# A right factor's cast and its difference given separate places in the order of work

## The chip, the cores and the metric

The kernel runs on one core of a Trainium2 chip. The metric is the time of one execution in device microseconds (us). One execution was also taken with the hardware profiler; its rows are in microseconds from the start of its span. PE is TensorE (matmuls), PEld its weight loads, DVE is VectorE, ACT is ScalarE, POOL is GpSimd and SP is SyncE.

## The reference, cut to what matters

A decoder layer in float32, on x of 1 x 512 x 2048: four token mixers with gates and an output projection, then an MLP of width 8192. The change lies in the MLP.

```python
def mlp(h, g, w_up, w_down):            # condensed; h: 512 x 2048
    y = rms_norm(h, g)
    u = jnp.square(jax.nn.relu(y @ w_up))   # 2048 -> 8192
    return h + u @ w_down                   # 8192 -> 2048
```

## The kernel before, in words

**Products.** Each float32 matmul is done as three products of rounded parts: of every operand there is a high part (a cast to the matmul's format) and a low part (the operand less its high part). `mm3` issues high by high, low by high and high by low (line 173, 128x128 weights by 128x256).

**Pairs.** The large multiplications use seven products of half size in place of eight (Winograd's form of Strassen's method). A *pair* makes one 256-row block of the result's channels from eight *keys* (pieces of the contraction), in seven products, in the order 1, 6, 7, 4, 5, 2, 3; a product is 8 keys x 3 = 24 matmuls. Four banks of PSUM, a to d, take the products: 1 in a, 6 in b, 7 in c, 4 in b again, 5 in d, then 2 on top of a, and 3 on top of d. VectorE adds each bank into the results when it is done (`add`, line 933: `ud<-pdb,y` reads product 6 out of bank b, `ud<-pdc` product 7, then into `y`), and ScalarE copies bank a (line 951). Product 4 can't start in b before `ud<-pdb,y` has been done.

**Left factors** are the weights: DMAs issued by SyncE bring quarters (`wq`), VectorE forms the method's sums (`z`, line 671), ScalarE casts them (`uh`, line 713) and VectorE makes the low part (`ul`, line 719). Each has three buffers.

**Right factors** are the activations, one of 7 x 256 columns for each key. `hi` is a cast on ScalarE (`sh`, line 886), `lo` a difference on VectorE (`sl`, line 890); `parts_of` returns the two steps. In up, the factors of keys 0 to 7 are made once, and hold for all 32 pairs. Up's results go through `hidden` (scale and ReLU on VectorE, square on ScalarE, four sums `token_sums` on VectorE at lines 858 to 861) and are written to memory as `zd` by GpSimd's DMA queue, as down's right factors. Down's pair n uses keys n to n + 7, so each pair needs one new right factor; it is fetched back (`std<-zd`, from GpSimd's queue) and made one pair ahead of its use, into one of nine slots. The next fetch is issued right behind the difference.

**Duos.** The first and the last two pairs of up and the first two of down go in two halves of the contraction (`run_duo`), so that keys 0 to 3 (of both pairs) come before keys 4 to 7. There, products share groups and left factors are 128x512.

**The order.** The order in which instructions are written is the order in which each engine runs them. `step` runs one product, and ahead of it what the planner gives: the cast of the left factor two products on, then all tasks from the list `later` that are due and marked `must`, then the difference of that left factor; then the product's matmuls; the reading of its bank is put in the list `pending` and comes at the next step. `wait_for(fn, n, after, must)` puts a task in `later`, due `after` microseconds on the planner's own clock, which goes by the matmuls planned. If a product needs a right factor that isn't made, `flush` takes the tasks in the order of their times until it is. The fetch of a later key's factor into slot 8 and the pair results share room in memory with the duos' results: slot 8's low part lies where the second pair's result `y1` was, which a GpSimd DMA adds to `x1d` (line 1325).

```python
    def in_parts(key, src, after=0.0, must=False, then=None):
        first, second = parts_of(key, src)
        ...
        wait_for(first, 0, after, must)
        wait_for(last, 7 * H, after, must)
    ...
    def place_down(J, after, following):
        in_parts(("d", J), staged[J], after, True, lambda: fetch_down(following))
    ...
            renew((n + 8,), (1.4,), (n + 9,))
```

Of the kernel before, what the change touches and what calls it, by code (L numbers as in the profile page):

```python
# [98 lines left out]
def body(nc, tc, ctx, dram):  # L99
# [25 lines left out]
    def t512(tag, name, dt=F32, rows=P):  # L125
        return stage[tag].tile([rows, S], dt, name=name, tag=tag, bufs=BUFS[tag])

    def bank(name, tag="mm"):
        return psum.tile([P, 512], F32, name=name, tag=tag, bufs=4)
# [109 lines left out]
    def pc(name, i=0, rows=P):  # L239
        c = _COLS[name][0] + i  # L240
        return par[:rows, c : c + 1]
# [369 lines left out]
    H = 256  # L611
# [139 lines left out]
    def spend(n):  # L751
        busy[0] += (0.06 + n / 960) / 1.09
# [19 lines left out]
    def wait_for(fn, n=0, after=0.0, must=False):  # L772

        later.append((clock[0] + after, n, fn, era[0], must))
# [23 lines left out]
    def result(name, where, tag, cols):  # L798

        for t in list(later):  # L800
            if t[3] < era[0]:
                pop(t)
        era[0] += 1
        return wide(name, where, tag, 2, cols)
# [49 lines left out]
    def token_sums(t):  # L854


        b11, b12, b21, b22, t2, t3, t4 = (t[:, q * H : (q + 1) * H] for q in range(7))
        V.tensor_tensor(out=t3, in0=b22, in1=b12, op=ALU.subtract)
        V.tensor_tensor(out=b12, in0=b12, in1=b11, op=ALU.subtract)
        V.tensor_tensor(out=t2, in0=b22, in1=b12, op=ALU.subtract)  # L860
        V.tensor_tensor(out=t4, in0=b21, in1=t2, op=ALU.subtract)
# [14 lines left out]
    def parts_of(key, src):  # L876


        def first():
            slot = slot_of(key)  # L880
            hi, lo = (
                spools[slot][1].tile([P, 7 * H], F32R, name=f"s{q}{key[0]}{key[1]}", tag=f"s{q}{slot}", bufs=1)
                for q in "hl"
            )
            place[key] = (hi, lo)
            A.copy(hi, src)  # L886

        def second():
            hi, lo = place[key]
            V.tensor_tensor(out=lo, in0=src, in1=f(hi), op=ALU.subtract)  # L890
            right[key] = (hi, lo)

        return first, second

    def in_parts(key, src, after=0.0, must=False, then=None):
        first, second = parts_of(key, src)

        def last():
            second()
            if then:  # L900
                then()

        wait_for(first, 0, after, must)
        wait_for(last, 7 * H, after, must)

    def fetch(key, where):

        t = wide(f"st{key[0]}{key[1]}", *where)
        G.dma_start(t, zd[key[0]][key[1] % UP])
        return t  # L910

    def wide(name, where, tag, bufs, cols=7 * H):
        return where[1].tile([P, cols], F32, name=name, tag=tag, bufs=bufs)

    def half_wide(name, where):
        return wide(name, where, "u", 1, S)
# [11 lines left out]
    def blocks(out, u):  # L928
        return [out[:, q * H : (q + 1) * H] for q in range(4)] + [u[:, :H], u[:, H:]]
# [69 lines left out]
    for k in range(4):  # L999
# [51 lines left out]
        for j in range(8):  # L1051
            for e, ps in rows(f"branch{k}", 0, j, yk, f"pb{k}"):
                n = 2 * j + e
# [56 lines left out]
    def gate_tiles(n):  # L1110
        j, k = GATES[n]
        return result(f"g{k}_{j}", gpool, "r", 1024), half_wide(f"u{k}_{j}", gpool)

    for n, phase in enumerate(gate_pairs):
        g, u = gate_tiles(n)
# [44 lines left out]
    for e in range(2):  # L1160
        hi, lo = (t512("q", f"mg{q}{7 + 8 * e}", F32R) for q in "hl")
        src = merged[0][:, e * S : (e + 1) * S]
# [9 lines left out]
    factors = {}  # L1172

    def add_in(out, a, b):
        V.tensor_tensor(out=out, in0=a, in1=b, op=ALU.add)

    def residual(n, ps):

        j, e = n % 8, n // 8
        r = t512("r", f"x1_{n}")  # L1180
        G.dma_start(r, dram["xT"][n])

        def first():
            spend(S)
            add_in(r, ps, r)
            G.dma_start(x1d[j][:, e * S : (e + 1) * S], r)
            wait_for(scaled, S, 0, n == 15)
            wait_for(square)

        def square():  # L1190
            sq = acc if n == 0 else t512("g", f"sq{n}")
            A.activation(sq, r, AF.Square)
            if n:
                wait_for(lambda: add_in(acc, acc, sq), S)

        def scaled():
            if e == 0:
                factors[j] = wide(f"x2_{j}", *((st1, "st1", 1) if j % 2 else (opool, "o", 1)))
            o = factors[j]
            V.scalar_tensor_tensor(  # L1200
                out=o[:, e * S : (e + 1) * S], in0=r, scalar=pc("g_mlp", n), in1=p, op0=ALU.mult, op1=ALU.mult,
            )
            if e:
                wait_for(sums, 4 * 300, 0, j == 7)

        def sums():
            token_sums(factors[j])
            if j < 4:
                in_parts(("u", j), factors[j])
            elif j < 6:  # L1210
                G.dma_start(zd["u"][j], factors[j])
            elif j == 7:
                in_parts(("u", 6), factors[6], 0, True)
                in_parts(("u", 7), factors[7], 5, True)

        return [first]

# [18 lines left out]
    last = {n: bank(f"pw{n}") for n in (7, 15)}  # L1236
# [28 lines left out]
    def up_tiles(n):  # L1265
        return result(f"h{n}", upool[0], "o", 7 * H), half_wide(f"uu{n}", upool[0])

    def hidden(n, o):
        up_scale = scale[1]
        if n == 0:  # L1270
            finish(scale[0])
            V.tensor_tensor(out=up_scale, in0=up_scale, in1=n2[1], op=ALU.mult)

        def scaled(e):
            r = o[:, e * S : (e + 1) * S]
            V.scalar_tensor_tensor(out=r, in0=r, scalar=0.0, in1=up_scale, op0=ALU.max, op1=ALU.mult)

        def sums():
            token_sums(o)
            G.dma_start(zd["d"][n], o)  # L1280

        for e in range(2):
            wait_for(lambda e=e: scaled(e), S)
        wait_for(lambda: A.activation(o[:, R], o[:, R], AF.Square))
        wait_for(sums, 4 * 300)
# [8 lines left out]
    staged = {}  # L1294

    def fetch_down(J):
        if J < UP + 7:
            staged[J] = fetch(("d", J), (upool[0], "s", 1) if J % 2 and J < 10 else ST1)

    def place_down(J, after, following):  # L1300
        in_parts(("d", J), staged[J], after, True, lambda: fetch_down(following))

    def renew(keys, times, following):
        for J, t, m in zip(keys, times, following):
            wait_for(lambda J=J, m=m: place_down(J, 0, m), 0, t, True)

    for n, phase in enumerate(up_pairs, 2):
        o, u = up_tiles(n)
# [2 lines left out]
            fetch_down(1)  # L1311
        run_pair(phase, o, u)
        hidden(n, o)
    TIMES = (0, 2.5, 11, 15)
    run_duo(
        up_last, [lambda n=n: up_tiles(n) for n in (UP - 2, UP - 1)],
        lambda: renew((0, 1, 2, 3), TIMES, (2, 3, 4, 5)),
        [lambda o, n=n: hidden(n, o) for n in (UP - 2, UP - 1)],
# [4 lines left out]
    def put(n, r):  # L1323
        q = n % 8
        G.dma_start(x1d[q], r, accum_op=ALU.add)
        if n >= UP - 8:
            for e in range(2):
                nc.sync.dma_start(dram["out"][q + 8 * e], x1d[q][:, e * S : (e + 1) * S])

    renew((4, 5, 6, 7), TIMES, (6, 7, 8, 9))  # L1330
    run_duo(
# [9 lines left out]
    for n, phase in enumerate(down_pairs, 2):  # L1341
        r, u = result(f"y{n}", dpool, "r", 1024), half_wide(f"ud{n}", dpool)
        if n + 1 < UP:
            renew((n + 8,), (1.4,), (n + 9,))
            run_pair(phase, r, u)
            pending.append(lambda n=n, r=r: put(n, r))
            continue
        x1 = wide("x1r", *ST1)[:, R]
        G.dma_start(x1, x1d[n % 8])
        x11, x12, x21, x22, _, _ = blocks(x1, u)  # L1350
        c11, c12, c21, c22, u2, u3 = blocks(r, u)

        def out(e, sl):
            nc.sync.dma_start(dram["out"][n % 8 + 8 * e][:, sl], r[:, e * S : (e + 1) * S][:, sl])

        run_pair(phase, r, u, {
            7: lambda: add_in(u2, u2, x12),
            4: lambda: add_in(c21, c21, x21),
            5: lambda: (add_in(c22, c22, x22), out(1, slice(0, S))),
            2: lambda: (add_in(c11, c11, x11), out(0, slice(0, H))),  # L1360
            3: lambda: out(0, slice(H, S)),
        })
# [77 lines left out]
```

## Time and profile before

| | |
|---|---|
| median of 3 runs | 2805.49 us (2804.15 to 2807.04) |
| the profiled execution's own time | 2807.36 us |
| its span, first to last instruction | 2805.6 us |
| mean granted TensorE clock | 0.993 |
| PE, PEld busy | 2722.6 us (97%), 2547.5 us (91%) |
| DVE, ACT, POOL busy | 2162.5 us (77%), 1229.7 us (44%), 180.4 us (6%) |

A busy share is an average over stages. In a row of the timeline stand the start, the duration, the engine, the line, the operation, what it writes and reads without buffer numbers, its shape, and in square brackets how long the engine had been idle and what ended that. The MLP's up begins at about 1452 us, down at about 2090, and down's steady pairs run from about 2206 to the end.

### The profile page before, as it was taken

The page shows a single profiled execution, that of the slowest core. Times are in us where ns is not written, and L with a number is a line of the kernel's source. Part 1 is how long each engine was busy: PE and PEld are TensorE (multiplying, and loading weights), DVE is VectorE, ACT ScalarE, POOL GpSimd, SP SyncE. Part 2 cuts the span into 40 slices and gives each one's busy share as a digit, 9 for nine tenths or more (in the row PEclk, how much of TensorE's full clock was granted, in tenths as well). Part 3 has the DMA queues.
Part 4 walks back from the last instruction along what each step waited for, and adds up shares of the span by engine and source line. Part 5 has one row for each costly group of instructions (what it writes and reads, how often), then busy time and mean ns, then how long its engine had stood idle before and what let it go on. Part 6 is the DMA issues. An engine that isn't in the chain of part 4 may idle for free. (4 is left out here: it accounts for less than half of the span.)

```text
span 2805.6 us, 48202 instructions
## 1 busy us (share of the span) xinstructions
PE 2722.6 (97%) x19904; PEld 2547.5 (91%) x19904; DVE 2162.5 (77%) x2664; ACT 1229.7 (44%) x1520; POOL 180.4 (6%) x298
## 2 busy tenths in 40 slices
PE   8999999999999999999999999999997999999999
PEld 7787777789999999998879999999997899999999
DVE  6875655577888888886559898888888787787786
ACT  5443334554444444443234444444444444444443
POOL 3000000000000000012100000000000000000000
PEclk9999999999999999999999999999998999999999
DMA  5232223564444444456444444444445555655564
GB/s 177 93 98 79 88 67 116 195 221 146 156 143 156 145 151 136 144 174 224 157 137 171 146 158 158 153 159 146 164 159 180 159 178 162 174 174 164 172 206 136
DMA packets 143901, 429.49 MB, mean 153 GB/s; under 512 B 16696, under 2 KB 30904, under 8 KB 143680
## 3 DMA queue, kind: packets, MB, share of 16 engines
q1 hardware_dynamic: 101536, 279.19, 29.5%
q0 software_dynamic: 32496, 129.65, 16.0%
q10 hardware_dynamic: 9648, 17.57, 1.7%
q8 instruction: 156, 2.56, 0.4%
q14 instruction: 65, 0.53, 0.1%
HBM read 350.04 MB, written 79.97 MB: 153 GB/s over the span
## 5 line engine op out<-in xcount | busy, mean ns | idle before, releaser
L713 ACT CAST uhd<-wqd 128x1024 fp32r<-128x1024 f32 (+3 forms) x136 | 135.4, 998 | 220.0 <-PE pdd L173 76.0
L713 ACT CAST uhg<-wqg 128x1024 fp32r<-128x1024 f32 (+1 forms) x136 | 135.6, 1000 | 185.3 <-PE pgd L173 96.4
L713 ACT CAST uhu<-wqu 128x1024 fp32r<-128x1024 f32 (+1 forms) x144 | 136.2, 952 | 163.5 <-PE pud L173 86.7
L151 DVE TENSOR_TENSOR wl<-wr,wh 128x1024 fp32r<-128x1024 f32 (+2 forms) x100 | 121.6, 1219 | 90.3 <-ACT wh L150 86.4
L719 DVE TENSOR_TENSOR ulg<-wqg,uhg 128x1024 fp32r<-128x1024 f32 (+1 forms) x136 | 157.1, 1158 | 33.4 <-ACT uhg L713 33.4
L713 ACT CAST uhd<-zd 128x1024 fp32r<-128x1024 f32 (+3 forms) x102 | 102.0, 1000 | 159.0 <-PE pdb L173 95.5
L150 ACT CAST wh<-wr 128x1024 fp32r<-128x1024 f32 (+2 forms) x100 | 101.1, 1014 | 160.3 <-PE pb L173 34.1
L719 DVE TENSOR_TENSOR uld<-wqd,uhd 128x1024 fp32r<-128x1024 f32 (+3 forms) x136 | 157.1, 1158 | 17.8 <-ACT uhd L713 17.8
L713 ACT CAST uhg<-zg 128x1024 fp32r<-128x1024 f32 (+1 forms) x102 | 102.0, 1000 | 150.0 <-DVE ulg L719 103.3
L173 PE MATMUL pdb<-shd,uhd 128*128 128x256 f32 x480 | 137.8, 287 | 30.0 <-DVE ud L933 30.0
L890 DVE TENSOR_TENSOR sld<-std,shd 128x1792 fp32r<-128x1792 f32 x39 | 78.9, 2025 | 111.9 <-ACT shd L886 105.8
L719 DVE TENSOR_TENSOR ulu<-wqu,uhu 128x1024 fp32r<-128x1024 f32 (+1 forms) x144 | 157.8, 1101 | 9.1 <-ACT uhu L713 9.0
L713 ACT CAST uhu<-zu 128x1024 fp32r<-128x1024 f32 (+1 forms) x108 | 103.1, 955 | 128.7 <-DVE ulu L719 69.0
L173 PE MATMUL pdb<-shd,uld 128*128 128x256 f32 x480 | 135.7, 283 | 0.0
L173 PE MATMUL pdb<-sld,uhd 128*128 128x256 f32 x480 | 135.6, 282 | 0.0
L173 PE MATMUL pda<-shd,uld 128*128 128x256 f32 x480 | 134.7, 281 | 0.8 <-DVE uld L719 0.8
L173 PE MATMUL pdd<-shd,uhd 128*128 128x256 f32 x480 | 134.6, 280 | 0.0
L173 PE MATMUL pdd<-shd,uld 128*128 128x256 f32 x480 | 134.5, 280 | 0.0
L173 PE MATMUL pda<-sld,uhd 128*128 128x256 f32 x480 | 134.5, 280 | 0.0
L173 PE MATMUL pda<-shd,uhd 128*128 128x256 f32 x480 | 134.5, 280 | 0.0
L173 PE MATMUL pdd<-sld,uhd 128*128 128x256 f32 x480 | 134.5, 280 | 0.0
L173 PE MATMUL pgb<-shg,ulg 128*128 128x256 f32 x480 | 134.2, 280 | 0.0
(1462 smaller groups left out, 10522.8 us busy)
## 6 DMA issues: line engine op xcount, KB each, us to landing
wqg<-in_w SPq DMA_DIRECT2D x120, 512.0 KB, 3.5
wqu<-in_w SPq DMA_DIRECT2D x112, 512.0 KB, 3.5
wr<-in_w SPq DMA_DIRECT2D x84, 512.0 KB, 3.5
std<-zd POOLq DMA_DIRECT2D x39, 896.0 KB, 4.8
zd<-h POOLq DMA_DIRECT2D x32, 896.0 KB, 4.8
bk<-b ACTq DMA_DIRECT2D x64, 256.0 KB, 2.8
b<-bk POOLq DMA_DIRECT2D x32, 512.0 KB, 4.6
wo<-in_w SPq DMA_DIRECT2D x32, 512.0 KB, 3.5
```

Of the source, the lines that this page charges most:

```text
L150: A.copy(hi, raw)
L151: V.tensor_tensor(out=lo, in0=raw, in1=f(hi), op=ALU.subtract)
L173: T.matmul(out, w, x, start=start, stop=stop, skip_group_check=more)
L713: A.copy(self.hi[:, sl], self.phase.source(i))
L719: V.tensor_tensor(out=lo, in0=self.phase.source(i), in1=f(hi), op=ALU.subtract)
L890: V.tensor_tensor(out=lo, in0=src, in1=f(hi), op=ALU.subtract)
```

## The change

`in_parts` gets an argument `apart`: the difference is due so much later than the cast. For down's right factors and up's last two it is 1, so that the difference comes one step after the cast. Up's keys 6 and 7 are made 2 us later (2 and 7 in place of 0 and 5), and the sums ahead of them as well. In down's first duo the last of four factors is due at 13 in place of 15. In pair 2 the new factor (key 10) is due at 9 in place of 1.4.

```diff
-    def in_parts(key, src, after=0.0, must=False, then=None):
+    def in_parts(key, src, after=0.0, must=False, then=None, apart=0.0):
...
         wait_for(first, 0, after, must)
-        wait_for(last, 7 * H, after, must)
+        wait_for(last, 7 * H, after + apart, must)
...
             if e:
-                wait_for(sums, 4 * 300, 0, j == 7)
+                wait_for(sums, 4 * 300, 2 if j == 7 else 0, j == 7)
...
             elif j == 7:
-                in_parts(("u", 6), factors[6], 0, True)
-                in_parts(("u", 7), factors[7], 5, True)
+                in_parts(("u", 6), factors[6], 2, True, None, 1)
+                in_parts(("u", 7), factors[7], 7, True, None, 1)
...
-        in_parts(("d", J), staged[J], after, True, lambda: fetch_down(following))
+        in_parts(("d", J), staged[J], after, True, lambda: fetch_down(following), 1)
...
-    TIMES = (0, 2.5, 11, 15)
+    TIMES = (0, 2.5, 11, 13)
...
         if n + 1 < UP:
-            renew((n + 8,), (1.4,), (n + 9,))
+            renew((n + 8,), (9 if n == 2 else 1.4,), (n + 9,))
```

No engine gets more or fewer instructions. Three places show what moves; a name's last number is a running one, and the one before it (if there are two) the key or the product.

VectorE in a steady pair (14) of down, before. `uld14_7`, `uld14_4` and `uld14_5` are the low parts of the left factors of products 7, 4 and 5; `sld22` is the right factor's difference:

```order
L719 TENSOR_TENSOR uld14_7_24941<-wqd14_0_1_24837,uhd14_7_24940 128x1024
L890 TENSOR_TENSOR sld22_24975<-std22_24744,shd22_24974 128x1792
L719 TENSOR_TENSOR uld14_4_24971<-wqd14_0_2_24840,uhd14_4_24970 128x1024
L933 TENSOR_TENSOR ud14_24935<-pdb_24937,y14_24934 128x256
L719 TENSOR_TENSOR uld14_5_25006<-zd14_1_24843,uhd14_5_25005 128x1024
L933 TENSOR_TENSOR ud14_24935<-pdc_24938,ud14_24935 128x256
```

VectorE in the same pair after the change:

```order
L719 TENSOR_TENSOR uld14_7_24941<-wqd14_0_1_24837,uhd14_7_24940 128x1024
L719 TENSOR_TENSOR uld14_4_24971<-wqd14_0_2_24840,uhd14_4_24970 128x1024
L933 TENSOR_TENSOR ud14_24935<-pdb_24937,y14_24934 128x256
L890 TENSOR_TENSOR sld22_24975<-std22_24773,shd22_24974 128x1792
L719 TENSOR_TENSOR uld14_5_25003<-zd14_1_24843,uhd14_5_25002 128x1024
L933 TENSOR_TENSOR ud14_24935<-pdc_24938,ud14_24935 128x256
```

The difference stands behind the low part for product 4 and the reading of bank b, and still ahead of the low part for product 5; the cast on ScalarE stays where it was.

VectorE in pair 2, the first whole pair of down, before:

```order
L719 TENSOR_TENSOR uld2_7_22139<-wqd2_0_1_22052,uhd2_7_22138 128x1024
L890 TENSOR_TENSOR sld10_22171<-std10_21859,shd10_22170 128x1792
L719 TENSOR_TENSOR uld2_4_22167<-wqd2_0_2_22055,uhd2_4_22166 128x1024
L933 TENSOR_TENSOR ud2_22133<-pdb_22135,y2_22132 128x256
L719 TENSOR_TENSOR uld2_5_22202<-zd2_1_22058,uhd2_5_22201 128x1024
```

VectorE there after the change:

```order
L719 TENSOR_TENSOR uld2_7_22139<-wqd2_0_1_22052,uhd2_7_22138 128x1024
L719 TENSOR_TENSOR uld2_4_22167<-wqd2_0_2_22055,uhd2_4_22166 128x1024
L933 TENSOR_TENSOR ud2_22133<-pdb_22135,y2_22132 128x256
L719 TENSOR_TENSOR uld2_5_22196<-zd2_1_22058,uhd2_5_22195 128x1024
L933 TENSOR_TENSOR ud2_22133<-pdc_22136,ud2_22133 128x256
L671 TENSOR_TENSOR zd2_2_22084<-wqd2_0_3_22226,zd2_2_22084 128x1024
L719 TENSOR_TENSOR uld2_2_22225<-wqd2_0_3_22226,uhd2_2_22224 128x1024
L933 TENSOR_TENSOR y2_22132<-pdb_22135,ud2_22133 128x256
L671 TENSOR_TENSOR zd3_1_22270<-wqd3_0_1_22264,wqd3_0_2_22267 128x1024
L719 TENSOR_TENSOR uld2_3_22258<-zd2_2_22084,uhd2_3_22257 128x1024
L933 TENSOR_TENSOR y2_22132<-pdd_22137,ud2_22133 128x256
L890 TENSOR_TENSOR sld10_22262<-std10_21908,shd10_22261 128x1792
```

Key 10's difference goes from the place behind product 7's low part to behind the reading of bank d after product 5; its cast moves on ScalarE in the same way, and GpSimd's fetch for key 11 follows it.

VectorE ahead of the second half of down's first duo, which begins with key 4 and takes key 7 for the first time, before. `h30` and `h31` are up's last two results, `sld7` is key 7's difference:

```order
L861 TENSOR_TENSOR h30_21287<-h30_21287 128x256
L890 TENSOR_TENSOR sld7_21818<-std7_21617,shd7_21817 128x1792
L671 TENSOR_TENSOR zd0_1_21737<-wqd0_0_2_21734,zd0_1_21737 128x512
L719 TENSOR_TENSOR uld0_5_21814<-zd0_1_21737,uhd0_5_21813 128x512
L719 TENSOR_TENSOR uld0_5_21814<-wqd0_0_2_21734,uhd0_5_21813 128x512
L933 TENSOR_TENSOR ud0_21812<-pd6_21566,y0_21811 128x256
```

VectorE there after the change:

```order
L861 TENSOR_TENSOR h30_21287<-h30_21287 128x256
L671 TENSOR_TENSOR zd0_1_21737<-wqd0_0_2_21734,zd0_1_21737 128x512
L719 TENSOR_TENSOR uld0_5_21817<-zd0_1_21737,uhd0_5_21816 128x512
L719 TENSOR_TENSOR uld0_5_21817<-wqd0_0_2_21734,uhd0_5_21816 128x512
L1276 SCALAR_TENSOR_TENSOR h31_21425<-h31_21425,ups_14263 128x512 x2
L858 TENSOR_TENSOR h31_21425<-h31_21425 128x256
L859 TENSOR_TENSOR h31_21425<-h31_21425 128x256
L860 TENSOR_TENSOR h31_21425<-h31_21425 128x256
L861 TENSOR_TENSOR h31_21425<-h31_21425 128x256
L890 TENSOR_TENSOR sld7_21795<-std7_21655,shd7_21794 128x1792
L933 TENSOR_TENSOR ud0_21815<-pd6_21566,y0_21814 128x256
```

The difference of key 7 goes behind a sum and two low parts of the left factors and behind h31's scaling and sums, and h31's work comes ahead of where it was.

## The prediction

> **What bounds the kernel now.** I read the page first, then TensorE's waits, then windows by stage, and last the rows of one pair on each engine. From the page:
>
> ```profile
> span 2805.6 us, 48202 instructions
> ...
> PE 2722.6 (97%) x19904; PEld 2547.5 (91%) x19904; DVE 2162.5 (77%) x2664; ACT 1229.7 (44%) x1520; POOL 180.4 (6%) x298
> ```
>
> TensorE is busy for 97% of the span, so no reordering can win more than the 83.0 us (2805.6 − 2722.6) in which it idles, and what it runs at half clock behind idle stretches. Its waits (line waited for, total us, times, longest):
>
> ```profile
> PE pdb L173 <- DVE ud L933: 30.0, 29, 5.2
> PE pu L173 <- DVE ulu L719: 12.4, 7, 3.8
> ```
>
> The largest is VectorE's reading of bank b in down's pairs, 29 times. Up's and down's steady stretches as windows (start:end, length, then busy us of PE, weight loads, VectorE, ScalarE, GpSimd, granted clock, DMA share, GB/s):
>
> ```profile
> 1530.00:2060.00 530.00, 529.78 (x4520) 529.58 (x4519) 469.93 (x597) 237.91 (x273) 14.88 (x28) 1.00 0.47 158
> 2206.00:2785.00 579.00, 555.07 (x4655) 550.34 (x4655) 454.27 (x473) 257.54 (x275) 38.89 (x55) 1.00 0.59 174
> ```
>
> In up VectorE is busy for 89% and TensorE never waits; in down VectorE has less to do (78%), and TensorE idles for 23.9 us. So the lack is one of order. One steady pair (14) on the four engines (start, us, operation, idle before):
>
> ```profile
> 2429.38 0.28 PE L173 MATMUL pdb<-shd,uhd 128*128 128x256 f32 x1
> 2432.22 0.28 PE L173 MATMUL pdc<-shd,uhd 128*128 128x256 f32 x1
> 2436.09 0.36 PE L173 MATMUL pdb<-shd,uhd 128*128 128x256 f32 x1 [0.87 <-DVE ud L933]
> ...
> 2429.51 1.05 ACT L713 CAST uhd<-wqd 128x1024 fp32r<-128x1024 f32 x1 [1.78 <-PE pda L173]
> ...
> 2430.72 1.69 ACT L886 CAST shd<-std 128x1792 fp32r<-128x1792 f32 x1
> ...
> 2427.76 1.23 DVE L719 TENSOR_TENSOR uld<-wqd,uhd 128x1024 fp32r<-128x1024 f32 x1 [0.58 <-ACT uhd L713]
> 2432.44 2.02 DVE L890 TENSOR_TENSOR sld<-std,shd 128x1792 fp32r<-128x1792 f32 x1 [3.46 <-ACT shd L886]
> 2434.39 1.22 DVE L719 TENSOR_TENSOR uld<-wqd,uhd 128x1024 fp32r<-128x1024 f32 x1
> 2435.52 0.42 DVE L933 TENSOR_TENSOR ud<-pdb,y 128x256 f32<-128x256 f32 x1
> 2435.85 1.22 DVE L719 TENSOR_TENSOR uld<-zd,uhd 128x1024 fp32r<-128x1024 f32 x1
> ```
>
> TensorE runs product 6 into bank b from 2429.38, product 7 into c from 2432.22, and wants b again for product 4 at 2435.05 (2432.22 plus 2.83, below). Bank b is full at about 2432.2, but VectorE reads it (ud<-pdb) only at 2435.52: it waited 3.46 us for the cast of the right factor, then made that factor's difference (2.02) and uld4 (1.22). ScalarE does the cast (shd) last of its work there, so VectorE idles in front of an operation that nobody needs before the next pair.
>
> **The change, part by part.**
>
> *Down's steady pairs, 3 to 30.* The stalls in question, first and last of 28, and the last pair, which makes no right factor (chain of waits):
>
> ```profile
> 2205.80 0.36 PE L173 MATMUL pdb<-shd,uhd 128*128 128x256 f32 x1 [0.88 <-DVE ud L933]
> 2770.87 0.36 PE L173 MATMUL pdb<-shd,uhd 128*128 128x256 f32 x1 [0.88 <-DVE ud L933]
> ...
> 2785.30 2.83 PE pdb L173 x24
> ...
> 2799.47 2.84 PE pdd L173 x24
> ```
>
> A pair now takes (2770.87 − 2205.80)/27 = 20.93 us. Without a stall it takes seven products of (2799.47 − 2785.30)/5 = 2.834, so 19.84: 1.09 less (0.88 of idle, the rest in the slower products behind it). Afterwards uld4 and ud<-pdb stand ahead of the difference. I replay it: uld7 runs from 2427.76 as now; uld4 follows its cast, done at 2430.56, and ends by about 2431.8; ud<-pdb goes at about 2432.4, when bank b is full; the difference at 2432.75, as shd ends at 2432.41; uld5 behind it is done by 2435.9. Product 4 starts at 2435.05 unhindered; product 5, which needs uld5, at 2437.9 and would need the low part some 0.2 us on: 2.2 us to spare. That is what is late next, and it isn't late. The moved step also issues the next fetch of std on GpSimd's queue; it comes 0.3 us later in its pair, at about 2435.1, some 15 us before the next cast wants it (2430.72 + 19.84). Ends: nothing gained (the wait moves to uld5), and, with up's 530.00/4520 = 0.1173 us a matmul, 168 of them in 19.70, 1.23 a pair. I take the last pair's, which runs the same instructions: 28 × 1.09 = 30.5 us (0 to 34.4).
>
> *Pair 2, the first whole pair of down.* Here the wait is longer, since slot 8's low part lies on a buffer that the adding DMA of the previous result still reads (rows of VectorE and PE, the window behind the wait, and the fetch of a factor with its count, size and median us to landing):
>
> ```profile
> 2178.69 2.03 DVE L890 TENSOR_TENSOR sld<-std,shd 128x1792 fp32r<-128x1792 f32 x1 [6.06 <-DMA x1d<-y]
> 2182.33 0.55 PE L173 MATMUL pdb<-shd,uhd 128*128 128x256 f32 x1 [5.19 <-DVE ud L933]
> 2187.59 0.41 PE L173 MATMUL pdd<-shd,uhd 128*128 128x256 f32 x1
> 2182.30:2188.00 5.70, 5.67 (x26) 5.70 (x27) 3.79 (x5) 0.34 (x1) 0.00 (x0) 0.50 0.86 297
> ...
> std<-zd POOLq DMA_DIRECT2D x39, 896.0 KB, 4.8
> ```
>
> The stall costs 5.19, and product 4 behind it takes 5.26 (2187.59 − 2182.33) in place of 2.83, at a granted clock of 0.50: 5.19 + 2.43 = 7.6 us. Product 1 of this pair began at 2168.7 (2182.33 − 5.19 − 3 × 2.83), so that DMA was done 10.0 into it. With 9 in place of 1.4 the difference of key 10 goes behind product 5, from 14.6 to 16.6 (5 × 2.83, a reading of 0.42, 2.02), when the DMA is long done. The next key's fetch then goes out at 17.0 and lands at 21.8; its cast wants it at 24.0 (19.84 + 4.2, as in pair 14), so 2 us are to spare. Ends: 0 and 8.2; I take 7.6. The Trainium skill, "TensorE: Matmul & The Clock Gate", section "What's actually happening", holds that an idle window of about 3.4 us halves the clock until a window has been busy. By that rule the loss behind the stall is half a window, 1.7 us, so the term would be 6.9 and the sum 0.7 smaller; the trace agrees on the 0.50 but shows 2.43, and the row decides.
>
> *Down's first duo, and up's last (2058 to 2171).* Waits on TensorE, and what held them (a window first):
>
> ```profile
> 2126.00:2136.00 10.00, 3.21 (x18) 2.42 (x16) 8.84 (x12) 5.00 (x7) 1.06 (x2) 0.70 0.51 183
> ...
> 2133.83 0.58 PE L173 MATMUL pd<-shd,uhd 128*128 128x256 f32 x1 [2.69 <-ACT shd L886]
> 2135.89 0.58 PE L173 MATMUL pd<-sld,uhd 128*128 128x256 f32 x1 [1.48 <-DVE sld L890]
> 2152.73 0.38 PE L173 MATMUL pd<-shd,uhd 128*128 128x256 f32 x1 [1.11 <-ACT uhd L713]
> 2157.11 0.58 PE L173 MATMUL pd<-shd,uld 128*128 128x256 f32 x1 [3.88 <-DVE uld L719]
> ...
> 2130.11 1.06 ACT L1284 ACTIVATE h<-h 128x1024 f32<-128x1024 f32 x1
> ...
> 2133.81 2.03 DVE L890 TENSOR_TENSOR sld<-std,shd 128x1792 fp32r<-128x1792 f32 x1 [0.73 <-ACT shd L886]
> 2154.30 2.03 DVE L890 TENSOR_TENSOR sld<-std,shd 128x1792 fp32r<-128x1792 f32 x1
> 2158.49 0.37 ACT L979 COPY y<-pd 128x256 f32<-128x256 f32 x1 [3.60 <-DMA zd<-h]
> ```
>
> Three things happen. Key 7's difference (2133.81) is needed by the second half's first product. It falls behind two uld, h31's two scalings, ScalarE's square of h31 (as the 1.06 of h30) and four sums; since all of it is needed at once, 13 in place of 15 doesn't help. These operations run some 2.4 us earlier than now, and by my count of their durations the difference ends at about 2137.4 in place of 2135.84, 1.5 later. Key 9's difference (2154.30) no longer stands ahead of uld1_7, so 3.88 and 1.11 fall away; and h31's factor is written earlier, so the copy no longer waits 3.60. The 2.4 is what the same shift wins in the duo parts ahead. In all I get +5.1 for the start of pair 2; what then limits is the weights' DMA into pair 2. Ends: −4, if key 7's lateness costs a stretch at half clock as in pair 2 and the later gains are swallowed; +14, if all these waits go.
>
> *Up's first duo.*
>
> ```profile
> 1457.06 0.38 PE L173 MATMUL pu<-shu,ulu 128*128 128x256 f32 x1 [1.24 <-DVE ulu L719]
> 1464.03 0.39 PE L173 MATMUL pu<-shu,ulu 128*128 128x256 f32 x1 [3.76 <-DVE ulu L719]
> 1468.18 2.02 DVE L890 TENSOR_TENSOR slu<-x,shu 128x1792 fp32r<-128x1792 f32 x1 [1.67 <-ACT shu L886]
> 1471.47 0.38 PE L173 MATMUL pu<-shu,ulu 128*128 128x256 f32 x1 [1.40 <-DVE ulu L719]
> ```
>
> Here slu6 and slu7 go 2 us later, behind the left factors that TensorE waits for. The three waits are 6.4 us; the same differences must be made before the second half, so half comes back: +3.0, between −1 and +6.9.
>
> Sum: 30.5 + 7.6 + 5.1 + 3.0 = 46.2 us. The profiled execution took 2807.36 us, 1.8 over its span; that gives 2761.2. It stands 1.87 above the median of the runs, 2805.49, so on their scale 2759.
>
> **The rivals.**
>
> *Key 7 goes worse than I count* (chance 0.15). Its difference now waits for h31's square and sums; TensorE idles up to 10 us there, and runs the next products at 0.50. The first duo's term is then −4: gain 37, 2768. For it: 5.19 of idle in pair 2 cost 2.43 behind it. Against: that stretch idles now too: 3.21 us busy in 10, clock 0.70.
>
> *The wait moves to uld5* (0.10). If the difference starts later than I replay, by more than 2.2 us, product 5 waits for uld5. At half of the old price a pair keeps 0.5: 14 us less gain, 2773. For it: VectorE has no pause from 2432.44 on, so each delay reaches uld5. Against: the 2.2 us, more than the difference itself takes.
>
> *All of it goes* (0.08): products at up's 0.1173 a matmul and the duos at their upper ends: 34.4 + 8.2 + 8 + 5 = 56, 2750. For it: up's pairs run so with VectorE busier. Against: the last pair, with no difference in it, ran at 2.834.
>
> *Slower: the right factor's fetch comes late* (0.03). In each pair ScalarE's cast of std stands ahead of the cast of uhd5; if std hasn't landed, ScalarE and then TensorE stand.
>
> ```profile
> DVE sld L890 <- ACT shd L886: 105.8, 35, 3.5
> ```
>
> Against it: the fetch lands 4.8 us after its issue, and 35 of VectorE's waits in front of the difference end on the cast. The cast would have to come 2.5 us later for a stall, and 4.2 (2.5, the 1.09 saved, and 16/28 for the other terms) for the kernel to be slower than before: std landing about 20 us after its issue (2435.1 to 2454.8). It is issued on GpSimd while VectorE works without a gap; the Trainium skill, "SBUF — State Buffer", section "SBUF: two separate sides", has VectorE and GpSimd share one port pair as an exclusive lock, which could hold up such an issue, and no run here shows it doing so.
>
> *No change* (0.02): the order shows the differences behind ud<-pdb; only a wait not in the trace could undo that.
>
> **How the numbers follow.** The forecast has 0.62: 2759, by itself 2752 to 2765 (the ends of the two duos). The range for 8 in 10 reaches on one side to the rival "all of it", 2749, and on the other past key 7's and half into uld5's, 2773. Faster by over 0.2% (5.6 us, about what a measurement of this kernel can tell) holds all cases but the last two: 0.95; same 0.02, slower 0.03.
>
> **What would show it.** Right: TensorE's wait on ud at L933 falls from 29 times 30.0 us to under 3; VectorE's idle time in front of sld falls from 105.8; a steady pair takes 19.8 to 19.9. Pair 2 shows no granted clock of 0.50. Key 7's sld ends later against the start of its half, and the wait for it grows. Wrong: waits on uld at L719 in every pair (then the second rival), or on uhd at L713 behind a late std.

## The result, and the profile after

The changed kernel takes 2759.56 us (median of 4 runs, 2758.59 to 2761.39), the kernel before 2804.82 (4 runs, 2804.07 to 2807.04): a ratio of 0.9834, 95% interval 0.9821 to 0.9847, 45.3 us less. The forecast was 2759. From the page of the profile after:

```profile
span 2756.7 us, 48177 instructions
...
PE 2709.0 (98%) x19904; PEld 2540.5 (92%) x19904; DVE 2163.2 (78%) x2664; ACT 1229.9 (45%) x1520; POOL 180.8 (7%) x298
```

The counts of instructions are the same on every engine and the busy times nearly so; the span is 48.9 us shorter. TensorE's longest waits after the change, then two of VectorE's (waited for, total us, times, longest):

```profile
PE pd L173 <- DVE sld L890: 11.1, 2, 10.3
PE pu L173 <- DVE ulu L719: 9.9, 5, 4.0
...
PE pd L173 <- DVE uld L719: 2.3, 4, 1.0
...
DVE ud L933 <- ACT shd L886: 18.4, 28, 0.7
...
DVE sld L890 <- ACT shd L886: 0.7, 1, 0.7
```

The line that headed the list before, bank b's reading with 30.0 us in 29 waits, is gone, and VectorE's idle time in front of the difference has fallen from 105.8 us to 0.7. New at the top is one wait of 10.3 us on `sld`: key 7's. The steady stretch as a window, and a steady pair on PE, ScalarE and VectorE:

```profile
2180.00:2733.00 553.00, 552.83 (x4690) 552.63 (x4689) 457.48 (x474) 261.11 (x279) 39.52 (x56) 1.00 0.63 185
...
2404.89 0.29 PE L173 MATMUL pdb<-shd,uhd 128*128 128x256 f32 x1
...
2400.56 1.70 ACT L886 CAST shd<-std 128x1792 fp32r<-128x1792 f32 x1
...
2400.42 1.23 DVE L719 TENSOR_TENSOR uld<-wqd,uhd 128x1024 fp32r<-128x1024 f32 x1 [1.60 <-ACT uhd L713]
2402.31 0.42 DVE L933 TENSOR_TENSOR ud<-pdb,y 128x256 f32<-128x256 f32 x1 [0.66 <-ACT shd L886]
2402.77 2.02 DVE L890 TENSOR_TENSOR sld<-std,shd 128x1792 fp32r<-128x1792 f32 x1
2404.71 1.22 DVE L719 TENSOR_TENSOR uld<-zd,uhd 128x1024 fp32r<-128x1024 f32 x1
```

TensorE now idles for 0.2 us in 553. VectorE reads bank b at 2402.31, and product 4 starts in it at 2404.89, with no idle time in its row. (The "0.66 <-ACT shd" before `ud<-pdb` is time in which VectorE waits for bank b to fill; the row names what ended about then.) The difference goes next, without a wait, and the low part for product 5 ends at 2405.93 (2404.71 plus 1.22), 2.0 us ahead of the matmul that takes it first, at 2407.95.

Where the 48.9 us are, by the starts of the first matmul into each stage's banks in the two traces:

| stage | before | after | gained | forecast |
|---|---|---|---|---|
| ahead of up | 1452.60 | 1451.16 | 1.4 | 0 |
| up's first duo | 50.08 | 47.42 | 2.7 | 3.0 |
| up's pairs | 555.61 | 555.48 | 0.1 | 0 |
| up's last and down's first duo | 109.14 | 103.58 | 5.6 | 5.1 |
| pair 2 | 28.82 | 20.85 | 8.0 | 7.6 |
| pairs 3 to 30 | 586.04 | 554.96 | 31.1 | 30.5 |
| pair 31 and after | 23.3 | 23.3 | 0 | 0 |

The profile of before was at the long end of its runs and that of after at the short end, so the two traces differ by some 3.5 us more than the medians do. The 1.4 us ahead of up are not the change's: in the twelve profiles of this document, whose code there is the same, up starts between 1450.3 and 1453.1 us. Down's first matmul is at 2104.86 us in the trace of before and at 2100.88 in that of after.

### The profile page after: what moved, and what is told of

It is laid out like the page before. It is cut to its first block, busy times and chain, and to the rows that moved or that the text cites. A ratio compares the mean times of both kernels' runs of the same rounds, so it can differ in the third digit from the quotient of the medians.

```text
span 2756.7 us, 48177 instructions
## 1 busy us (share of the span) xinstructions
PE 2709.0 (98%) x19904; PEld 2540.5 (92%) x19904; DVE 2163.2 (78%) x2664; ACT 1229.9 (45%) x1520; POOL 180.8 (7%) x298
## 5 line engine op out<-in xcount | busy, mean ns | idle before, releaser
L713 ACT CAST uhg<-wqg 128x1024 fp32r<-128x1024 f32 (+1 forms) x136 | 135.6, 999 | 185.3 <-PE pgd L173 96.4
L173 PE MATMUL pgd<-shg,ulg 128*128 128x256 f32 x480 | 134.2, 280 | 0.0
```

The source lines that it names most:

```text
L173: T.matmul(out, w, x, start=start, stop=stop, skip_group_check=more)
L713: A.copy(self.hi[:, sl], self.phase.source(i))
```

## The experiments

Each kernel was also profiled, and is read by the same stages.

**The steady pairs alone.** The kernel before, and a difference one step behind the cast for keys 11 and up:

```diff
-        wait_for(last, 7 * H, after, must)
+        wait_for(last, 7 * H, after + apart, must)
...
+        in_parts(("d", J), staged[J], after, True, lambda: fetch_down(following), 1 if J > 10 else 0)
```

> The kernel before with the difference one step behind the cast in pairs 3 to 30 alone. Theory (the steady pairs lose 1.09 us each because the difference stands ahead of the reading of bank b): a pair takes 19.82 in place of 20.93, TensorE's waits on ud at L733's successor L933 fall from 29 to 1 (pair 2's, still about 5.2), the duos and pair 2 stay as before, and the time is 31 us under before, about 2774. Rival (the gain in the pairs needs the other parts too, or the wait moves to the low part of product 5): over 20.2 us a pair and waits on uld in every pair, time above 2783.

Its time was 2775.74 us (before, on the same chip: 2803.97). The pairs 3 to 30 took 554.50 us, 19.80 each. TensorE's waits on bank b's reading:

```profile
PE pdb L173 <- DVE ud L933: 5.4, 1, 5.4
```

One wait is left of 29, pair 2's. So this part does its 31 us without the others, as the theory had it. The time is only 28.2 us less, since the two duos, left as they were, took 111.25 us in this execution (109.14 in the profile of before).

**The cast moved in place of the difference.** The kernel before, where in pairs 3 to 30 the cast is due at once and the difference at 1.4:

```diff
+        in_parts(("d", J), staged[J], after, True, lambda: fetch_down(following), 1.4 if J > 10 else 0)
...
-            renew((n + 8,), (1.4,), (n + 9,))
+            renew((n + 8,), (1.4 if n == 2 else 0,), (n + 9,))
```

> The kernel before with the cast of the right factor one step earlier in pairs 3 to 30, ahead of the cast for product 4's left factor, the difference where it was. Theory (what was late was VectorE's 3.5 us wait for ScalarE's cast, so parting the two is what counts, whichever is moved): the difference ends at about 4.8 us into the pair, bank b is read at 5.9 and wanted at 8.5; a pair takes 19.8 to 19.9 and the time is 30 us under before, about 2774. Rival (only a difference behind the reading of bank b helps): the 0.88 wait on ud stays at 0.4 or more in each pair, time above 2785.

2774.43 us (before: 2805.95); 19.80 a pair. A pair on ScalarE and VectorE:

```profile
2413.87 1.69 ACT L886 CAST shd<-std 128x1792 fp32r<-128x1792 f32 x1
...
2415.59 2.03 DVE L890 TENSOR_TENSOR sld<-std,shd 128x1792 fp32r<-128x1792 f32 x1 [0.37 <-ACT shd L886]
2417.53 1.22 DVE L719 TENSOR_TENSOR uld<-wqd,uhd 128x1024 fp32r<-128x1024 f32 x1
2418.72 0.42 DVE L933 TENSOR_TENSOR ud<-pdb,y 128x256 f32<-128x256 f32 x1
```

Here the difference still stands ahead of the reading of bank b, and nothing waits: VectorE idles for 0.37 us in front of it in place of 3.46. The stall came from the time in which VectorE stood waiting for ScalarE, not from the 2.02 us of the difference. Parting the two is what counts; in the steady pairs it matters little which of them is moved.

**How much room product 5 has.** The kernel after, with the difference written twice, and three times, in pairs 3 to 30:

```diff
             V.tensor_tensor(out=lo, in0=src, in1=f(hi), op=ALU.subtract)
+            if key[0] == "d" and key[1] > 10:
+                V.tensor_tensor(out=lo, in0=src, in1=f(hi), op=ALU.subtract)
             right[key] = (hi, lo)
```

> The kernel after, with the right factor's difference done twice in each of the pairs 3 to 30 (the second writes the same values; 1.94 us more VectorE work at that place). Theory (the low part for product 5 has 2.1 us to spare in the trace of after): a pair still takes 19.8 to 19.9, no waits over 0.2 us, time within 4 us of after, about 2760. Rival (the gain is VectorE's idle time, of which a pair has little left): each pair longer by 0.5 to 1.9.

> The kernel after, with the difference done three times in pairs 3 to 30 (3.88 us more). Theory: the low part for product 5 comes 1.8 us too late in each pair, TensorE waits on uld at L719 (bank d) 28 times for about 1.75 us, a pair takes 21.6 and the time is 49 us over after, about 2808. Rival (the work is what counts, VectorE then has 19.3 of 19.8 us to do): under 0.5 a pair, below 2775.

Written twice: 2769.84 us, 20.13 a pair, 0.31 more than after, so neither theory's number. VectorE's low part for product 5, and TensorE's matmuls around its use:

```profile
2412.22 1.22 DVE L719 TENSOR_TENSOR uld<-zd,uhd 128x1024 fp32r<-128x1024 f32 x1
...
2413.28 0.28 PE L173 MATMUL pdd<-sld,uhd 128*128 128x256 f32 x1
2413.49 0.39 PE L173 MATMUL pdd<-shd,uld 128*128 128x256 f32 x1
```

The low part ends at 2413.44, the matmul that needs it starts 0.21 after the one ahead in place of 0.12. The room was used up to within 0.1 us; over the 28 pairs products 5, 2 and 3 each lose 0.08 to 0.10 and the next pair's product 1 loses 0.06, in pieces too short to be listed as waits. Written three times: 2853.09 us, 23.13 a pair (waits, and a window over most of the pairs):

```profile
PE pdd L173 <- DVE uld L719: 52.5, 28, 2.0
...
2206.00:2800.00 594.00, 545.16 (x4304) 539.27 (x4303) 524.45 (x487) 240.85 (x257) 35.77 (x51) 0.94 0.55 159
```

The waits come where they were expected, 28 of them, and of the expected size (52.5/28 = 1.88, expected 1.75). What the expectation left out is the clock: it was granted at 0.94 over these pairs, which is some 36 us more ((1 − 0.94) × 594). The room was 2.0 us, where the replay had 2.2. VectorE's total of work was not the limit: with 1.94 us more of it a pair grew by only 0.31.

**Pair 2.** Key 10 made at 9 without any other part of the change, and all of the change without that 9:

```diff
# the kernel before, with
-            renew((n + 8,), (1.4,), (n + 9,))
+            renew((n + 8,), (9 if n == 2 else 1.4,), (n + 9,))
# the kernel after, with
-            renew((n + 8,), (9 if n == 2 else 1.4,), (n + 9,))
+            renew((n + 8,), (1.4,), (n + 9,))
```

> The kernel before with key 10's factor due at 9 in place of 1.4 in pair 2 alone, cast and difference together. Theory (the wait of pair 2 is the adding DMA's hold on slot 8): pair 2 takes about 20.9 in place of 28.8, the 5.2 us wait and the half clock behind it go, all else stays; time 8 us under before, about 2797. Rival (the difference stalls wherever it goes, because it stands in front of VectorE's other work): the wait moves to a later product of pair 2 and most of the 8 us stays.

> The kernel after with 1.4 for every pair, so key 10's difference comes behind the reading of bank b but before the adding DMA is done. Theory (the DMA holds slot 8 until 10.0 us into the pair): VectorE stands in front of the difference until then, the difference ends 12.0 and the low part for product 5 13.2 into the pair, which product 5 wants at 11.5: a wait of about 1.7 on uld at L719, pair 2 takes 22.6 in place of 20.9, time 2 us over after. Rival (one step behind the cast is enough here as in the other pairs): 20.9 and no difference from after.

The first took 2804.26 us (before: 2803.97), so its time shows nothing; its pair 2 took 22.82 (expected: 20.9), 6.0 less than in the profile of before, and other stretches were longer in that execution than in that profile (1.4 in down's first duo, 1.0 in up's pairs, whose code is the same). VectorE and TensorE:

```profile
2185.45 2.03 DVE L890 TENSOR_TENSOR sld<-std,shd 128x1792 fp32r<-128x1792 f32 x1 [2.17 <-ACT shd L886]
...
2190.23 0.36 PE L173 MATMUL pdd<-shd,uhd 128*128 128x256 f32 x1 [1.75 <-DVE y L933]
```

The DMA no longer holds the difference, but cast and difference together do what they did in the steady pairs: VectorE waits 2.17 us for the cast, and TensorE 1.75 for a reading behind it. The rival had that wait, the theory the larger part. The second took 2759.51 us, as after; its pair 2 took 22.61, as expected, with a wait of 1.29 (expected: 1.7):

```profile
2168.15 2.03 DVE L890 TENSOR_TENSOR sld<-std,shd 128x1792 fp32r<-128x1792 f32 x1 [3.37 <-ACT uhd L713]
...
2171.37 0.39 PE L173 MATMUL pdd<-shd,uld 128*128 128x256 f32 x1 [1.29 <-DVE uld L719]
```

The row of the difference names a cast that ended at about that time, but the difference doesn't use that cast; the adding DMA, issued at 2161.73, landed at 2168.03, and the difference began at 2168.15.

So against the profile of before either edit alone takes 6 of the 8 us, and the 9, with the difference parted from its cast, is worth the last 1.8. The 8 is at the upper end: pair 2 as it was took 28.82 us in that profile, but 27.39 and 26.89 in the two runs with only the steady pairs changed. With both edits it took 20.15 to 20.92 in seven profiles, so by the means (27.7 and 20.7) the two are worth 7.0 us together, and each alone about 5.

**The duos as before.** The kernel after, keys 0 to 9 made as before, 15 in place of 13:

```diff
+        in_parts(("d", J), staged[J], after, True, lambda: fetch_down(following), 1 if J > 9 else 0)
...
+    TIMES = (0, 2.5, 11, 15)
```

> The kernel after with down's keys 0 to 9 made as before (cast and difference together, 15 in place of 13 for the last of the duo's four). Theory (the duo's part of the change gains 5.6 net, in spite of a wait of 10.3 on key 7's difference): from the end of up's last duo to the start of pair 2 it takes 62.6 as before in place of 56.8, the 10.3 us wait is gone and the waits of 2.6, 2.7, 1.5 and 3.9 are back; time 5 to 6 us over after, about 2765. Rival (key 7's long wait costs more than the duo gains elsewhere, and the gain there comes from up's first duo or from the pairs): the same time as after or less.

2766.34 us, 6.8 over after. The two duos took 111.04 us in place of 103.58 (down's alone 64.49, expected 62.6), the wait of 10.3 is gone, and that on uld1_7 is back:

```profile
2155.72 0.58 PE L173 MATMUL pd<-shd,uld 128*128 128x256 f32 x1 [3.88 <-DVE uld L719]
```

The duos' part is a gain, in spite of its new wait. Of that wait, in the trace of after (PE, then VectorE):

```profile
2122.30 0.39 PE L173 MATMUL pd<-shd,uhd 128*128 128x256 f32 x1
2132.97 0.58 PE L173 MATMUL pd<-sld,uhd 128*128 128x256 f32 x1 [10.28 <-DVE sld L890]
...
2129.18 0.42 DVE L858 TENSOR_TENSOR h<-h 128x256 f32<-128x256 f32 x1 [1.12 <-ACT h L1284]
...
2130.89 2.02 DVE L890 TENSOR_TENSOR sld<-std,shd 128x1792 fp32r<-128x1792 f32 x1
```

TensorE stands for key 7's low part from 2122.7, and VectorE comes to it at 2130.89, after h31's sums. Can this wait be taken away too?

**Key 7 earlier.** The kernel after with 12.5 in place of 13, which puts key 7's difference right behind key 6's:

> The kernel after with 12.5 in place of 13 for the duo's last factor, so that key 7's difference comes right behind key 6's and not behind h31's square and sums. Theory (the 10.3 us wait comes from the place of that difference): the wait falls to about 1.2 us, the half clock behind it goes; from the start of down to pair 2 it takes 49 to 53 in place of 56.8, as h31's factor is then written later and the copy of the second pair's result waits some 3 us for it; time about 2754. Rival (what limits there is the weights' DMA or the factors' fetches, so the wait only moves): within 1 us of after's 56.8.

```profile
2123.62 0.39 PE L173 MATMUL pd<-sld,uhd 128*128 128x256 f32 x1 [1.31 <-DVE sld L890]
2136.91 0.58 PE L173 MATMUL pd<-shd,uld 128*128 128x256 f32 x1 [5.54 <-DVE uld L719]
...
2134.69 0.37 ACT L979 COPY y<-pd 128x256 f32<-128x256 f32 x1 [6.88 <-DMA zd<-h]
...
2127.03 0.54 POOL L1280 DMA_DIRECT2D zd<-h  x1 [2.65 <-DVE h L861]
```

2761.61 us, no gain on after (2759.56): the expectation failed. The wait on key 7 did fall, from 10.28 to 1.31. But ScalarE's copy of y0, the first result of down, stands from 2127.8 to 2134.69: it is written where h30 was, and h30's way to memory was issued at 2127.03, behind two fetches on GpSimd's queue, and took 7.6 us. In the kernel after, the 10.3 us wait had hidden this one. From the start of down to pair 2 it took 60.25 us (after: 56.76 in its first profile, 61.05 in a second one, below).

**And h30's work earlier.** The same, with fixed times for the work on up's last two results, so that h30's sums come ahead of key 6's difference:

```diff
+    DUE = {30: (0, 6, 15.5), 31: (15, 15, 17)}
...
+        due = DUE.get(n, (0, 0, 0))
...
-            wait_for(lambda e=e: scaled(e), S)
-        wait_for(lambda: A.activation(o[:, R], o[:, R], AF.Square))
-        wait_for(sums, 4 * 300)
+            wait_for(lambda e=e: scaled(e), S, due[0], n in DUE)
+        wait_for(lambda: A.activation(o[:, R], o[:, R], AF.Square), 0, due[1], n in DUE)
+        wait_for(sums, 4 * 300, due[2], n in DUE)
...
+    TIMES = (0, 2.5, 11, 12.5)
```

> The kernel of the run before this (key 7's difference early, 12.5) with the work on up's last two results given fixed places: h30's square and sums ahead of key 6's difference, h31's scaling behind product 7's low parts and its sums behind the reading of bank 6. Theory (in that run the wait that took the place of key 7's was the copy of y0, which stands until h30 has been written to memory, 7.6 us after the issue): the write goes out some 10 us earlier, the copy no longer waits and the 5.5 us wait on uld0_3 goes; key 7's difference ends 1.8 later, a wait of about 3 us. From the start of down to pair 2 it takes 53 to 56 us; time 1 to 4 us under after, which a comparison of times can't show. Rival (VectorE's work in the duos is what limits, 94 of 110 us): 57 or more, the waits only move again.

GpSimd's write of h30 and ScalarE's copy of y0; then the window of both duos in this kernel, in after and in before:

```profile
2113.53 0.54 POOL L1283 DMA_DIRECT2D zd<-h  x1 [2.59 <-DVE h L861]
...
2127.05 0.37 ACT L979 COPY y<-pd 128x256 f32<-128x256 f32 x1
...
2053.03:2149.43 96.40, 86.11 (x674) 83.83 (x673) 89.47 (x138) 50.89 (x70) 7.25 (x13) 0.95 0.61 208
```

```profile
2054.05:2157.63 103.58, 84.22 (x674) 82.40 (x673) 89.57 (x138) 50.79 (x70) 7.27 (x13) 0.93 0.58 193
```

```profile
2058.29:2167.43 109.14, 86.87 (x674) 83.86 (x673) 90.30 (x139) 50.83 (x70) 7.28 (x13) 0.92 0.54 183
```

2751.24 us (4 runs, 2750.97 to 2753.70), ratio to before 0.9806 (0.9790 to 0.9823). The kernel after took 2758.00 in the same comparison (2756.14 to 2760.61): 6.8 us less, and the runs of the two don't overlap, though the intervals of their ratios to before do. The write goes out about 13 us earlier, the copy doesn't wait, and down's first duo takes 50.50 us, better than the 53 to 56 expected. The same 674 matmuls and the same work on VectorE now lie in 96.4 us, so VectorE's load (89.5 us) was not the limit there; the order was, and with it the clock (0.95 in place of 0.93).

**The kernel after once more.**

> The kernel after, unchanged, for the spread between executions. Theory (the same waits meet the clock gate in another phase each time): the steady pairs, up's first duo and pair 2 repeat within 0.1 us (19.82 a pair, 47.4, 20.9), the stretch of the last and first duos (103.6 in the profile of after) comes back within 1.5 us but not within 0.1. Rival (the waits themselves differ from run to run): the 10.3 us wait on key 7's difference differs by over 0.5.

19.83 a pair and 47.41 in up's first duo, as expected, and the wait on key 7 is 10.28 again. But the two duos took 107.08 in place of 103.58, more than the 1.5 expected, and pair 2 took 20.15 in place of 20.85. The same wait in the two executions, and the window behind it; first the profile of after, then this one:

```profile
2085.92 0.38 PE L173 MATMUL pu<-shu,ulu 128*128 128x256 f32 x1 [1.92 <-DVE ulu L719]
...
2086.00:2089.40 3.40, 3.40 (x29) 3.40 (x30) 3.40 (x8) 3.14 (x4) 0.00 (x0) 1.00 0.83 281
```

```profile
2085.08 0.39 PE L173 MATMUL pu<-shu,ulu 128*128 128x256 f32 x1 [1.93 <-DVE ulu L719]
...
2086.00:2089.40 3.40, 3.40 (x19) 3.40 (x18) 3.40 (x8) 2.54 (x4) 0.00 (x0) 0.53 0.80 292
```

One wait of 1.9 us is followed by a full clock in one execution and by half of it in the other: 29 matmuls in 3.40 us, and 19. In the stretch from up's last duo through pair 2 the half clock lasted 13.65 us in the first, and 20.47 in the second. That is 6.8 us more at half speed, worth 3.4 us of work, while the whole stretch took 2.8 us more (127.2 against 124.4). So the clock is large enough to account for the difference; that it is all of it isn't shown, as some waits changed as well (1.76 us on a low part at the end of down's first duo in the second, 0.26 in the first).

## Why the prediction was right

**The steady pairs** (30.5 forecast, 31.1 measured). The step held as a whole: the reading of bank b no longer waits, product 5 has 2.0 us to spare (forecast 2.2), the last pair's 2.834 a product is what all pairs now take (19.84 for seven of them; the pairs took 19.80 to 19.84 in all kernels with the two parted and the difference made once). The rival in which the wait moves to uld5 was ruled out by the margin, and the run with the difference written twice shows that margin to be real. Up's lower 0.1173 a matmul was not reached. The forecast said that the difference was moved out of the way; the run with the cast moved shows that the better statement is that VectorE no longer stands behind ScalarE.

**Pair 2** (7.6 and 8.0). The size was about right, its cause only in part. The step gave all of it to the 9, which takes the difference past the DMA. Measured one by one against the profile of before, the parting alone gives 6.2 us and the 9 alone 6.0; together they give 8.0, or 7.0 by the means over several profiles. The loss behind the stall, 2.43 in the forecast's row, depends on the execution: behind pair 2's wait the clock was at half for 6.83 us in the profile of before and for 3.41 in the two other runs with pair 2 as it was, worth 1.7 us of work, the price that the forecast named and set aside for its row. A reading was off too, though nothing came of it: product 1 of pair 2 began at 2167.43 and not at 2168.7, for it held a wait of 0.79 of its own, so the DMA was done 11 us into the pair and not 10.

**The duos** (5.1 and 5.6, by the two profiles). Key 7's difference ended 78.9 us after the start of up's last duo, before 77.6: 1.3 later, forecast 1.5. The gains behind it came as forecast: the 3.88, the 1.11 and the copy's 3.60 are gone. But the idle stretch of "up to 10 us", with products at half clock behind it, belonged to the rival that key 7 goes worse, and it came: 10.3 us, and half clock until 2136.17. What didn't come is that rival's price of −4, because the 10.3 us stand where waits of 2.34, 2.62, 2.69 and 1.48 us (9.1 together) stood before. That the agreement is to 0.5 us is luck: the forecast's 5.1 isn't added up from its parts (the differences alone, −1.5 + 3.88 + 1.11 + 3.60, are 7.1), and the stretch itself varies by more than 0.5. The kernels with the old order in the duos took 109.1, 111.3, 110.5, 111.0 and 110.7 us there, those with the new 103.6, 103.9, 104.2, 104.6 and 107.1. Their means are 110.5 and 104.7, so the term is 5.9, and one execution of it can be 2 or 3 off.

**Up's first duo** (3.0 and 2.7). Four kernels with the old order took 50.1 us, eight with the new 47.4, each within 0.02; this term was the roughest in its working and the steadiest in the trace. Of the three waits' 6.4 us 4.0 are left, and a new one of 0.7 on a left factor's cast has come; so the guess that half comes back was near in size and no more than that. Behind the 3.76 us wait the clock was at half for 3.41 us in two of the four and for 6.83 in the other two, and the stretch was equally long, since the third wait was the shorter for it (1.40 and 1.65 us, against 0.28 and 0.16): VectorE's order set the length there, and not TensorE's speed.

**The slower rival**, a late fetch of the right factor, did not come: the fetch landed a median 5.0 us after its issue, and no wait in the steady pairs names it. As to the port pair that VectorE and GpSimd would share, nothing in these runs shows an issue held up by it.

**What the sum left out** outside pair 2 is the clock. The rule cited for pair 2 (the Trainium skill, "TensorE: Matmul & The Clock Gate", section "What's actually happening") speaks of a free-running window of 4096 cycles, 3.4 us. The traces agree on its length: the half clock in the stretch above lasted 13.65, 20.47 and 10.24 us in after, its repetition and the kernel with h30's work early, which is 4, 6 and 3 times 3.41. They agree too that it is a matter of phase: in each trace, from up's last duo on, all starts and ends of half clock but the trace's own end lie on one grid of 3.413 us, and on it the wait of 1.93 us above falls whole into one window, while an edge cuts that of 1.92 us into 0.97 and 0.95. They don't bear out that such a window must be idle throughout: 1.9 us of it were enough, and in the kernel with the difference written three times, waits of 1.88 us brought the mean down to 0.94. Over all twelve traces (from 2053 to 2200 us, to 2800 in that kernel), every full-clock window with over 1.87 us of TensorE's idle time in it was followed by one at half, and none with under 1.66 was, so it takes about half a window. Windows at half were followed by full clock where they held at most 0.32 us of idle time, and by half again from 0.80 on.

## What to carry to other kernels

Where two engines make one thing in turn, and the second runs its instructions in order, put other work that is needed soon between the two steps: an engine that stands in front of an operation nobody needs yet holds up everything behind it. Then count the room of what is next in line, and lengthen the moved step to see whether the count is right. A long wait can hide another right behind it: here taking away 10.3 us gained nothing until the transfer that it had covered was moved as well.

## What was not expected of the hardware

A single wait of TensorE of 1.9 us can be followed by 3.4 us at half clock or by none, by its place against the clock's windows: whether about half of one window is idle decides. The same order of work gave a stretch of 103.6 and of 107.1 us, in good part by this. And an operand that arrives less than 0.1 us late is not listed as a wait: products 5, 2 and 3 took 2.91 to 2.93 us in place of 2.83 where VectorE was just at its limit.
